# Scan gates in float32, the mixing stage's GpSimd products on VectorE, and the output turned to token rows by TensorE

## The chip, the cores and the metric

One core of one Trainium2 chip runs the kernel in one launch. The metric is the device time of that core in microseconds (us). A core has TensorE (PE in the profile, with its weight loads as PEld), VectorE (DVE), ScalarE (ACT), GpSimd (POOL) and SyncE (SP), each with an instruction queue that it works off in order; here SP issues nearly all transfers. The engines meet at semaphores.

## The reference

One layer of a bidirectional encoder: 256 tokens, 2048 features, all in float32. `rms` is an RMS norm with a gain.

```python
x = x + 0.5 * swiglu(rms(x), w1_ffn1, w3_ffn1, w2_ffn1)      # hidden width 5632
proj = rms(x) @ w_in                                         # 2048 -> 3584
q, k, v, u, y = ...                                          # 8 / 2 / 2 heads of 128; u and y 1024 wide
q, k = rope(rms(q)), rope(rms(k));  A = attention(q, k, v)   # no mask
uc = centred_conv4(u)
for each direction:                                          # forward and backward
    r = sigmoid(blockdiag(uc, w_a) + b_a)                    # 8 blocks of 128 x 128
    i = sigmoid(blockdiag(uc, w_i) + b_i)
    log_a = -8 * softplus(-lambda) * r;  a = exp(log_a)
    h[t] = a[t] * h[t-1] + sqrt(1 - a[t]**2) * i[t] * uc[t]  # scan over the tokens
x = x + concat([A, (h_fwd + h_bwd) * gelu(y)]) @ w_out
x = x + 0.5 * swiglu(rms(x), w1_ffn2, w3_ffn2, w2_ffn2)
x = x + sigmoid(rms(x) @ w_gate) * (p @ w_ple)
return rms(x)
```

The output has one row of 2048 features for each token.

## The kernel before

All 256 tokens stay in SBUF as `xs`, with the features along the partitions (16 tiles of 128 features x 256 tokens). The weights are read once from HBM, 1 MB at a time, into `raw`, of which there are three (SP issues the loads, L103). Every weight product is made in pieces of reduced float32 (fp32r): `split` (L82) cuts a half of a weight tile, 128x1024, into a high part `whi` (a cast on ACT, L83) and a low part `wlo` (a subtraction on DVE, L84); TensorE multiplies whi by the high and low part of the activations (L115, 512 columns) and wlo by the high part (L117, 256 columns). There is a ring of four pairs of whi and wlo (`SPL`), so ACT and DVE can be at most some three halves ahead of TensorE. In `proj` (L152), which makes q, k and v, the activations stand still and the weights move: three matmuls of 512 columns (L91 to L93, `mm3`) for each of eight products with a half.

The stages are the first FFN (0 to about 755 us), the mixing stage (to 965), the output projection of the mixing with `wout` (to 1051), the second FFN (to 1782), the gate with the per-layer input (to 1878) and the tail. In the mixing stage the order is: four units of u and the conv for scan group 0, four for group 1, then k and v, then two projections of q, then eight units of y. Between them run jobs, which are Python generators: `tick` (L97) takes one step of each, once after a unit and once after a quarter of a projection. The jobs are: `scan_job` (from L375) for the gates, the scans (L424, along the tokens, 128x256 each, 16 in all) and their sum `hsum`; `k_job` and `q_job` for the transposes, scores, softmax and values of the attention; `y_job` for gelu, the product with hsum and the split into `mixT`, which is the input of wout.

In the scan job the gates use mm3 too: ACT and GpSimd split the conv's output `uc` and the gate weights, and TensorE makes three fp32r matmuls of 256 columns for each of 32 products. GpSimd further makes these elementwise products of the mixing stage: us times the norm (L437), the gate times the decay constant (L407), the input gate times uc (L413), their product with the square root (L421), the sum of the directions (L427), the cosine part of the rotation (L461), and y times the norm (L574). In the whole kernel it also has the power -0.5 of the norms (L210), some products of the FFN (L304, L246) and of the gate stage.

The code gives the order in which instructions are made; a scheduler of the tile framework, which simulates the engines, then sets the order in each engine's queue. A queue is then fixed, so an instruction that waits holds all behind it.

In the tail, features 14 and 15 of the gate are done in two halves of the tokens (L651). For each half the sums of squares go through TensorE (L219), the power on GpSimd, a diagonal (L231) and a matmul (L232) that lays the norms along the free axis; DVE and GpSimd multiply xs by them (L639) and SP writes ten transfers (L641) in pieces of 512 bytes. The host puts the output into token order.

## Time and profile before

| | |
|---|---|
| runs | 1907.08, 1907.63, 1908.33 us; median 1907.63 |
| profiled execution | 1907.39 us; its span is 1905.6 us |
| PE busy | 1872.7 us, 98% of the span |
| DVE busy | 1203.6 us, 63% |
| ACT busy | 965.2 us, 51% |
| POOL busy | 292.6 us, 15% |
| mean granted clock of TensorE | 0.993 |

The profile is of one execution, and 1.8 us lie outside its span. "Busy" is the time in which an instruction runs; TensorE is pipelined, and the record of a matmul runs on for some 0.2 us after the next one has begun, so the distance between starts is the price of a matmul in a row of them. "PEclk" is the clock that TensorE was granted: 1.00 is 2.4 GHz, 0.50 is 1.2 GHz.

### The profile page before, as it was taken

The numbers are of one execution on the slowest core, as the hardware profiler recorded it, in microseconds if no ns is written. First come the engines' busy times: TensorE is split into PE (matmuls) and PEld (weight loads), VectorE is DVE, ScalarE is ACT, GpSimd is POOL, SyncE is SP. The second block draws the span as 40 slices with busy tenths as digits, with TensorE's granted clock in tenths as the row PEclk, the third lists the DMA queues.
The fourth block names the chain that finished last, engine by engine and source line by source line (L and its number), as shares of the span: only waits on it lengthen the run. The fifth ranks groups of instructions, "written<-read, shape, count | busy, mean of one in ns | idle before, by whom it ended". The sixth has DMA issues, their size and how long they took to land.

```text
span 1905.6 us, 27228 instructions
## 1 busy us (share of the span) xinstructions
PE 1872.7 (98%) x10632; PEld 1640.3 (86%) x10632; DVE 1203.6 (63%) x1723; ACT 965.2 (51%) x1494; POOL 292.6 (15%) x225
## 2 busy tenths in 40 slices
PE   9999999999999999988999999999999999999997
PEld 7888888888888888867878888888888888888886
DVE  6766655556566556888767666655555666655686
ACT  6544444444444445677654544444444444555553
POOL 0111100011111001564211111110001111101143
PEclk9999999999999999999999999999999999999998
DMA  8555545655555556544345555555565555555552
GB/s 316 205 189 187 192 160 190 210 199 179 197 180 176 182 184 213 175 152 155 133 152 181 191 185 194 182 186 167 194 208 196 181 195 184 202 197 195 201 177 67
DMA packets 61552, 352.85 MB, mean 185 GB/s; under 512 B 6512, under 2 KB 12144, under 8 KB 31088
## 3 DMA queue, kind: packets, MB, share of 16 engines
q1 hardware_dynamic: 60848, 350.51, 54.0%
q8 instruction: 83, 1.36, 0.3%
q10 hardware_dynamic: 576, 0.61, 0.1%
q14 instruction: 45, 0.37, 0.1%
HBM read 349.00 MB, written 2.10 MB: 184 GB/s over the span
## 4 chain that ended last, share of the span: by engine, by line
PE 92%; DVE 3%; ACT 3%; issue 1%; POOL 1%; DMA 0%; SPq 0%; POOLq 0%; DVEq 0%; ACTq 0%
PE acc L115 59%; PE acc L117 30%; DVE wlo L84 1%; DVE gate L424 1%; DVE uc L370 0%; ACT whi L83 0%; PE po L522 0%; PE acc L656 0%; PE pe L115 0%; POOL us L437 0%; DMA xs<-in_xT 0%; PE tr L495 0%; ACT gate L403 0%; ACT a L410 0%; ACT L416 0%
## 5 line engine op out<-in xcount | busy, mean ns | idle before, releaser
L84 DVE TENSOR_TENSOR wlo<-raw,whi 128x1024 fp32r<-128x1024 f32 x722 | 806.5, 1126 | 594.7 <-ACT whi L83 577.5
L83 ACT CAST whi<-raw 128x1024 fp32r<-128x1024 f32 x722 | 687.0, 952 | 814.5 <-PE acc L115 553.9
L115 PE MATMUL acc<-aT,whi 128*128 128x512 f32 x3296 | 832.0, 393 | 1.2 <-DVE aT L88 1.2
L115 PEld LDWEIGHTS acc<-aT,whi 128*128 128x128 f32 x3296 | 593.1, 189 | 107.8 <-DVE aT L88 2.7
L117 PEld LDWEIGHTS acc<-aT,wlo 128*128 128x128 f32 x3296 | 451.4, 191 | 32.7
L117 PE MATMUL acc<-aT,wlo 128*128 128x256 f32 x3296 | 463.0, 283 | 0.0
L115 PE MATMUL acc<-hT,whi 128*128 128x512 f32 x1408 | 364.8, 392 | 0.0
L304 POOL TENSOR_TENSOR s<-s,rB 128x256 f32<-128x256 f32 x88 | 123.8, 1407 | 1067.7 <-ACT s L301 1061.9
L115 PEld LDWEIGHTS acc<-hT,whi 128*128 128x128 f32 x1408 | 247.6, 189 | 37.2
L117 PEld LDWEIGHTS acc<-hT,wlo 128*128 128x128 f32 x1408 | 202.7, 190 | 21.3
L117 PE MATMUL acc<-hT,wlo 128*128 128x256 f32 x1408 | 209.0, 282 | 0.0
L246 POOL TENSOR_TENSOR ssq<-ssq,sqr 128x256 f32<-128x256 f32 x58 | 54.4, 939 | 339.6 <-ACT sqr L245 339.6
L115 PE MATMUL acc<-mixT,whi 128*128 128x512 f32 x256 | 64.6, 393 | 1.4 <-DVE mixT L84 1.4
L115 PEld LDWEIGHTS acc<-mixT,whi 128*128 128x128 f32 x256 | 45.9, 189 | 10.2 <-DVE mixT L84 2.1
L315 DVE SCALAR_TENSOR_TENSOR xs<-acc,xs 128x256 f32<-128x256 f32 x128 | 53.3, 417 | 0.0
L87 ACT ACTIVATE aT<-xs,par_sb 128x256 fp32r<-128x256 f32 x64 | 31.5, 506 | 41.9 <-DVE xs L315 39.3
L92 PE MATMUL acc<-wlo,aT 128*128 128x512 f32 x96 | 40.4, 421 | 11.3 <-DVE wlo L84 11.3
L88 DVE SCALAR_TENSOR_TENSOR aT<-xs,par_sb,aT 128x256 fp32r<-128x256 f32 x64 | 38.2, 610 | 19.4 <-ACT aT L87 19.1
L306 DVE TENSOR_TENSOR u<-u,s 128x256 f32<-128x256 f32 x88 | 37.4, 426 | 9.1 <-DVE u L149 0.5
L93 PE MATMUL acc<-whi,aT 128*128 128x512 f32 x96 | 39.8, 415 | 0.0
L84 DVE TENSOR_TENSOR hT<-u,hT 128x256 fp32r<-128x256 f32 x88 | 38.0, 431 | 1.9 <-ACT hT L83 1.9
L300 DVE TENSOR_TENSOR z<-z,rB 128x256 f32<-128x256 f32 x88 | 37.4, 425 | 2.7
(168 smaller groups left out, 1001.5 us busy)
## 6 DMA issues: line engine op xcount, KB each, us to landing
raw<-in_w2a SPq DMA_DIRECT2D x64, 704.0 KB, 4.0
raw<-in_w1b SPq DMA_DIRECT2D x44, 1024.0 KB, 4.8
raw<-in_w3b SPq DMA_DIRECT2D x44, 1024.0 KB, 4.9
raw<-in_w2b SPq DMA_DIRECT2D x64, 704.0 KB, 4.0
raw<-in_w3a SPq DMA_DIRECT2D x43, 1024.0 KB, 4.8
raw<-in_w1a SPq DMA_DIRECT2D x42, 1024.0 KB, 4.8
raw<-in_win SPq DMA_DIRECT2D x16, 1024.0 KB, 4.9
raw<-in_wout SPq DMA_DIRECT2D x16, 1024.0 KB, 4.8
```

Source lines behind the costliest of these rows:

```text
L83: nc.scalar.copy(hi, src)
L84: (eng or nc.vector).tensor_tensor(lo, src, f32(hi), op=ALU.subtract)
L88: nc.vector.scalar_tensor_tensor(lo, src, gain, f32(hi), op0=ALU.mult, op1=ALU.subtract)
L92: nc.tensor.matmul(ps, lhsT=ah, rhs=wl, start=False, stop=False)
L93: nc.tensor.matmul(ps, lhsT=al, rhs=wh, start=False, stop=last)
L115: nc.tensor.matmul(ps, lhsT=ws[i][0], rhs=acts[i], start=first and i == 0, stop=False)
L117: nc.tensor.matmul(ps[:, 1, :], lhsT=ws[i][1], rhs=acts[i][:, 0, :], start=False, stop=last and i == n - 1)
L246: (eng or nc.gpsimd).tensor_tensor(ssq[:, cols], ssq[:, cols], t, op=ALU.add)
L300: nc.vector.tensor_tensor(z, z, rB, op=ALU.mult)
L304: nc.gpsimd.tensor_tensor(s, s, rB, op=ALU.mult)
L306: nc.vector.tensor_tensor(u, u, s, op=ALU.mult)
L315: nc.vector.scalar_tensor_tensor(xs[:, n, :], ps[:, j, :], 0.5, xs[:, n, :], op0=ALU.mult, op1=ALU.add)
```

## The change

Four things change.

The gates of the scans (L398 now) are one plain float32 matmul for each of the 32 products, straight from `uc` and the weights as loaded; the splits of uc and of the gate weights are gone. The gate weights come by two loads of 512 KB for each group into tiles of the pool `mid`, in place of one into `raw`.

All products that GpSimd made in the mixing stage are issued to DVE. GpSimd keeps the power of the norms there.

Jobs take smaller steps and more of them: `unit` ticks after each half of the weights, `proj` after every second product of a quarter, the scan job yields in more places, and y's job is cut in two. `finish` runs the jobs to their end at two places: until hsum of a group exists before that group's y units, and all jobs before the second half of the first wout unit. The rows of wout are stored in another order (MIX_ORDER: heads 0 to 3, scan group 0, heads 4 to 7, scan group 1), and mixT is read in that order.

In the tail both halves of the tokens are finished first. Then TensorE transposes xs (32 transposes, L685), ACT and DVE scale the PSUM tiles by the token's norm, which is now a scalar for each partition (L693, L691), and SP writes eight transfers of 256 KB in rows of 2 KB (L694). The output leaves in token order.

```diff
+MIX_ORDER = [*range(4), *range(8, 12), *range(4, 8), *range(12, 16)]
...
+    def finish(done=lambda: not jobs):
+        while not done():
+            tick()
...
     def unit(aT, srcs, nk, other=None, drain=None):
...
+                if at == drain:
+                    finish()
                 unit_mms(ps, part, aT[at:at + len(part)], at == 0, at + len(part) == n)
                 at += len(part)
-        tick()
+                tick()
...
     def proj(aT, srcs):
...
-            tick()
+                if k % 2:
+                    tick()
...
     def scan_job(g, u):
-        hi = mid.tile([P, 4, S], F32R, tag="mid", name="uc_hi")
-        lo = mid.tile([P, 4, S], F32R, tag="mid", name="uc_lo")
-        split(u, hi, lo, nc.gpsimd)
-        raw = wraw.tile([P, 4, C], F32, tag="raw", name="raw")
-        in_order(nc.sync.dma_start(flat(raw), lruw[g]), loads[-1])
-        yield
         gw = []
         for d in range(2):
-            wh = mid.tile([P, 2, C], F32R, tag="mid", name="gw_hi")
-            wl = mid.tile([P, 2, C], F32R, tag="mid", name="gw_lo")
-            split(raw[:, 2 * d:2 * d + 2, :], wh, wl, nc.gpsimd)
-            gw.append((wh, wl))
+            w = mid.tile([P, 2, C], F32, tag="mid", name="gw")
+            load(flat(w), lruw[g, :, 2 * C * d:2 * C * (d + 1)])
+            gw.append(w)
         yield
...
-                        mm3(ps[:, j, :], wh[:, m, wc], wl[:, m, wc], hi[:, k, :], lo[:, k, :],
-                            True, True)
+                        nc.tensor.matmul(ps[:, j, :], lhsT=gw[d][:, m, k * P:(k + 1) * P], rhs=u[:, k, :],
+                                         start=True, stop=True)
...
-            nc.gpsimd.tensor_tensor(r[d], r[d], cb, op=ALU.mult)
+            nc.vector.tensor_tensor(r[d], r[d], cb, op=ALU.mult)
+            yield
...
-            nc.gpsimd.tensor_tensor(flat(i[d]), flat(i[d]), flat(u), op=ALU.mult)
+            nc.vector.tensor_tensor(flat(i[d]), flat(i[d]), flat(u), op=ALU.mult)
...
-            nc.gpsimd.tensor_tensor(flat(r[d]), flat(r[d]), flat(i[d]), op=ALU.mult)
+            yield
+            nc.vector.tensor_tensor(flat(r[d]), flat(r[d]), flat(i[d]), op=ALU.mult)
+            yield
             for k in range(4):
...
+                if k % 2:
+                    yield
-        nc.gpsimd.tensor_tensor(flat(i[0]), flat(i[0]), flat(i[1]), op=ALU.add)
+        nc.vector.tensor_tensor(flat(i[0]), flat(i[0]), flat(i[1]), op=ALU.add)
...
-            nc.gpsimd.tensor_tensor(t, t, rmB, op=ALU.mult)
+            nc.vector.tensor_tensor(t, t, rmB, op=ALU.mult)
...
-        nc.gpsimd.tensor_tensor(sv, sv, cb, op=ALU.mult)
+        nc.vector.tensor_tensor(sv, sv, cb, op=ALU.mult)
...
     for g in range(2):
+        finish(lambda: hsum[g] is not None)
...
-            nc.gpsimd.tensor_tensor(y[:, k, :], t, rmB, op=ALU.mult)
-        jobs.append(y_job(g, y))
-
-    tick()
+            nc.vector.tensor_tensor(y[:, k, :], t, rmB, op=ALU.mult)
+            if k % 2:
+                jobs.append(y_job(g, k // 2, y[:, k - 1:k + 1, :]))
+
+    order = [mixT[k] for k in MIX_ORDER]
...
-        ps = unit(mixT, [wout[n, 0]], NKD)
+        ps = unit(order, [wout[n, 0]], NKD, drain=8 if n == 0 else None)
...
+    def in_rows(h, b):
...
+        for k in range(4):
+            nc.tensor.transpose(ps[:, k * P:(k + 1) * P], xs[:, 4 * b + k, h * P:(h + 1) * P], ident)
+        return ps
+
+    def put(h, b, ps, r):
+        o = tok.tile([P, C], F32, tag="att", name="out", bufs=ATT)
+        if b % 2:
+            nc.vector.tensor_scalar(o, ps, r, None, op0=ALU.mult)
+        else:
+            nc.scalar.activation(o, ps, AF.Copy, scale=r)
+        nc.sync.dma_start(out[h * P:(h + 1) * P, b * C:(b + 1) * C], o)
+
+    last_features(0)
+    last_features(1)
+    r0 = norms(0)
+    for b in range(4):
+        put(0, b, in_rows(0, b), r0)
+    ahead = [in_rows(1, b) for b in range(3)]
+    r1 = norms(1)
+    for b in range(3):
+        put(1, b, ahead[b], r1)
+    put(1, 3, in_rows(1, 3), r1)
```

The queues outside the mixing stage and the tail keep their order on every engine. In the queues below a number behind a name tells one buffer from another, and a name's last `<-` has what is read.

On DVE, before, at the projections of k, v and q: the gates of scan group 0 (`a` is the decay, `gate` the gates and, later, the scan's results) come in four rows of scans among the subtractions for the weights.

```order
L419 SCALAR_TENSOR_TENSOR gate_7240<-a_7496,gate_7240 128x1024
L419 SCALAR_TENSOR_TENSOR gate_7375<-a_7500,gate_7375 128x1024
L84 TENSOR_TENSOR wlo_7694<-raw_7691,whi_7693 128x1024
L424 SCALAR_TENSOR_TENSOR gate_7310<-a_7496,gate_7240 128x256 x4
L84 TENSOR_TENSOR wlo_7698<-raw_7691,whi_7697 128x1024
L424 SCALAR_TENSOR_TENSOR gate_7434<-a_7500,gate_7375 128x256 x4
L84 TENSOR_TENSOR wlo_7753<-raw_7750,whi_7752 128x1024
L209 TENSOR_SCALAR rs_v_7586<-qss_7581 128x2
L84 TENSOR_TENSOR wlo_7757<-raw_7750,whi_7756 128x1024
```

On DVE, after, at the same place; the products that GpSimd made stand among them (L414 and L407 of group 1, L423 of group 0).

```order
L88 TENSOR_TENSOR wlo_7574<-raw_7571,whi_7573 128x1024
L420 SCALAR_TENSOR_TENSOR gate_7128<-a_7421,gate_7128 128x1024
L414 TENSOR_TENSOR gate_7425<-gate_7425,uc_7080 128x1024
L423 TENSOR_TENSOR gate_7128<-gate_7128,gate_7190 128x1024
L420 SCALAR_TENSOR_TENSOR gate_7288<-a_7453,gate_7288 128x1024
L88 TENSOR_TENSOR wlo_7578<-raw_7571,whi_7577 128x1024
L427 SCALAR_TENSOR_TENSOR gate_7190<-a_7421,gate_7128 128x256 x4
L88 TENSOR_TENSOR wlo_7629<-raw_7626,whi_7628 128x1024
L423 TENSOR_TENSOR gate_7288<-gate_7288,gate_7348 128x1024
L88 TENSOR_TENSOR wlo_7633<-raw_7626,whi_7632 128x1024
L407 TENSOR_TENSOR gate_7500<-gate_7500,cneg_6844 128x1024
L427 SCALAR_TENSOR_TENSOR gate_7348<-a_7453,gate_7288 128x256 x2
```

Four scans still stand between two subtractions, and three more products of 128x1024 stand among six subtractions.

On PE, before, where wout begins (two units run side by side, acc_8662 and acc_8710): the transposes of the last softmax (`pt`, L513) and the values (`po`, L522) stand after the third of the eight pairs of input tiles of mixT. mixT_7618, which L115 reads in the last row, has heads 6 and 7, the outcome of po_8544.

```order
L115 MATMUL acc_8710<-mixT_7617,whi_8713 128x512 x2
L513 MATMUL tr_8475<-ident_102,pt_8409 128x128
L513 MATMUL tr_8482<-ident_102,pt_8409 128x128
L513 MATMUL tr_8475<-ident_102,pt_8421 128x128
L513 MATMUL tr_8475<-ident_102,pt_8409 128x128
L513 MATMUL tr_8475<-ident_102,pt_8421 128x128
L513 MATMUL tr_8482<-ident_102,pt_8421 128x128
L513 MATMUL tr_8482<-ident_102,pt_8409 128x128
L513 MATMUL tr_8482<-ident_102,pt_8421 128x128
L522 MATMUL po_8544<-pT_sb_8480,v_sb_7337 128x256 x2
L522 MATMUL po_8544<-pT_sb_8487,v_sb_7337 128x256 x2
L115 MATMUL acc_8662<-mixT_7618,whi_8665 128x512 x2
```

On PE, after, at the same place, with the values of heads 4 and 5 (po_8218) and the scores (L499) and transposes (L517) of heads 6 and 7; mixT_7561, 7562 and 7565 hold heads 0 to 3 and the first pair of scan group 0.

```order
L526 MATMUL po_8218<-pT_sb_8193,v_sb_7323 128x256 x2
L499 MATMUL tr_8225<-kT_7560,qT_8104 128x256 x2
L499 MATMUL tr_8237<-kT_7560,qT_8104 128x256 x2
L526 MATMUL po_8218<-pT_sb_8200,v_sb_7323 128x256 x2
L517 MATMUL tr_8280<-ident_102,pt_8231 128x128
L517 MATMUL tr_8287<-ident_102,pt_8231 128x128
L123 MATMUL acc_8574<-mixT_7565,whi_8577 128x512 x2
L123 MATMUL acc_8626<-mixT_7565,whi_8629 128x512 x2
L517 MATMUL tr_8280<-ident_102,pt_8243 128x128
L517 MATMUL tr_8280<-ident_102,pt_8231 128x128
L517 MATMUL tr_8280<-ident_102,pt_8243 128x128
L517 MATMUL tr_8287<-ident_102,pt_8243 128x128
```

Behind these rows stand two more transposes, four matmuls of the values of heads 6 and 7 (po_8314), and only then the unit goes on, with mixT_7566 (the second pair of scan group 0). What the first half of wout reads is no longer made by the last values, but the last values still stand ahead of it in PE's queue.

On DVE, before, at the very end: the norm of the first half (rs_v, dg), the last features, three products for the output, then the second half's norm and five more products.

```order
L231 TENSOR_SCALAR dg_17157<-ident_102,inv_17153 128x128
L615 TENSOR_TENSOR small_17097<-small_17097,pe_17036 128x128
L616 TENSOR_TENSOR xs_83<-xs_83,small_17097 128x128
L620 TENSOR_TENSOR last_17060<-xs_83 128x128
L639 TENSOR_TENSOR xs_83<-xs_83,rows_17161 128x4x128 x3
L621 TENSOR_SCALAR xs_83<-xs_83,par_sb_82 128x128
L209 TENSOR_SCALAR rs_v_17222<-sums_17217 128x1
L231 TENSOR_SCALAR dg_17225<-ident_102,inv_17221 128x128
L639 TENSOR_TENSOR xs_83<-xs_83,rows_17226 128x2x128 x2
L639 TENSOR_TENSOR xs_83<-xs_83,rows_17226 128x4x128 x3
```

On DVE, after, at the very end: four scalings of transposed tiles (`out`), of 128 tokens by 512 features each, wait for the norms and the transposes alone; ACT has the other four.

```order
L221 TENSOR_SCALAR rs_v_17122<-sums_17118 128x1
L662 TENSOR_TENSOR sqr_17113<-xs_83 128x128
L664 TENSOR_TENSOR last_16975<-last_16975,sqr_17113 128x128
L667 TENSOR_SCALAR xs_83<-xs_83,par_sb_82 128x128
L691 TENSOR_SCALAR out_17138<-out_17133,inv_17121 128x512
L691 TENSOR_SCALAR out_17154<-out_17149,inv_17121 128x512
L221 TENSOR_SCALAR rs_v_17176<-sums_17172 128x1
L691 TENSOR_SCALAR out_17182<-out_17162,inv_17175 128x512
L691 TENSOR_SCALAR out_17193<-out_17188,inv_17175 128x512
```

The diagonal and its matmul are gone, and no product waits for a GpSimd product.

## Rows read from the trace of the kernel before

**Rows 1.** Windows: busy us (and instructions) of each engine, clock, DMA share, GB/s.
```profile
core 0: us, PE busy (x) PEld busy (x) DVE busy (x) ACT busy (x) POOL busy (x), PEclk, DMA share, GB/s
830.00:893.00 63.00, 49.97 (x200) 38.99 (x201) 54.13 (x56) 40.56 (x77) 34.46 (x17) 0.89 0.34 117
951.00:965.00 14.00, 9.40 (x40) 6.75 (x40) 8.12 (x19) 10.33 (x20) 0.72 (x1) 0.88 0.22 75
965.00:1051.00 86.00, 86.00 (x498) 75.82 (x497) 60.88 (x77) 44.01 (x62) 13.96 (x14) 1.00 0.54 183
```

**Rows 2.** Waits of PE from 755 to 1051: total us, times, longest.
```profile
PE acc L92 <- DVE wlo L84: 11.3, 5, 4.7
PE tr L513 <- DVE pt L506: 2.3, 2, 1.8
```

**Rows 3.** Timeline, 829 to 846: start, us, engine, operation, idle before it.
```profile
831.01 1.21 DVE L84 TENSOR_TENSOR wlo<-raw,whi 128x1024 fp32r<-128x1024 f32 x1
831.23 3.23 POOL L421 TENSOR_TENSOR gate<-gate 128x1024 f32<-128x1024 f32 x1 [1.23 <-DVE gate L419]
832.14 6.74 DVE L424 TENSOR_TENSOR_SCAN gate<-a,gate 128x256 f32<-128x256 f32 x4
834.21 0.63 PE L92 MATMUL acc<-wlo,aT 128*128 128x512 f32 x1
834.64 0.63 PE L93 MATMUL acc<-whi,aT 128*128 128x512 f32 x1
...
839.92 2.42 DVE L424 TENSOR_TENSOR_SCAN gate<-a,gate 128x256 f32<-128x256 f32 x4
...
840.06 0.80 PE L92 MATMUL acc<-wlo,aT 128*128 128x512 f32 x1 [3.17 <-DVE wlo L84]
```

**Rows 4.** Timeline, 874 to 894: the scans of group 1.
```profile
875.27 6.69 DVE L424 TENSOR_TENSOR_SCAN gate<-a,gate 128x256 f32<-128x256 f32 x4
...
883.13 0.80 PE L92 MATMUL acc<-wlo,aT 128*128 128x512 f32 x1 [4.72 <-DVE wlo L84]
```

**Rows 5.** DVE's groups, 755 to 965: busy us, mean ns, idle before.
```profile
L84 DVE TENSOR_TENSOR wlo<-raw,whi 128x1024 fp32r<-128x1024 f32 x55 | 80.9, 1485 | 20.5 <-ACT whi L83 16.6 <-ACT pT_sb L515 2.0 <-ACT rB L236 1.5
L424 DVE TENSOR_TENSOR_SCAN gate<-a,gate 128x256 f32<-128x256 f32 x16 | 18.3, 1199 | 0.0
...
L419 DVE SCALAR_TENSOR_TENSOR gate<-a,gate 128x1024 f32<-128x1024 f32 x4 | 7.3, 1818 | 5.9 <-ACT gate L416 5.9
...
L149 DVE TENSOR_TENSOR ys<-acc,ys 128x256 f32<-128x256 f32 x8 | 3.4, 419 | 0.2
```

**Rows 6.** GpSimd's group L421 of the same stretch.
```profile
L421 POOL TENSOR_TENSOR gate<-gate 128x1024 f32<-128x1024 f32 x4 | 12.2, 3062 | 15.1 <-DVE gate L419 12.0 <-PE acc L93 3.1
```

**Rows 7.** ACT's groups of the same stretch.
```profile
L403 ACT ACTIVATE gate<-tr,par_sb 128x256 f32<-128x256 f32 x32 | 12.6, 477 | 0.0
...
L410 ACT ACTIVATE a<-gate 128x1024 f32<-128x1024 f32 x4 | 4.0, 1052 | 0.0
L403 ACT ACT_TABLE_LOAD x3 | 3.8, 1283 | 0.1
```

**Rows 8.** PE's timeline, 799.5 to 801.5: gate matmuls.
```profile
800.61 0.28 PE L91 MATMUL tr<-uc_hi,gw_hi 128*128 128x256 f32 x1
800.72 0.28 PE L92 MATMUL tr<-uc_lo,gw_hi 128*128 128x256 f32 x1
```

**Rows 9.** PE's timeline, 905 to 925: four float32 matmuls of the values, four of scores.
```profile
911.62 1.89 PE L522 MATMUL po<-pT_sb,v_sb 128*128 128x256 f32 x8
913.35 1.89 PE L495 MATMUL tr<-kT,qT 128*128 128x256 f32 x8
```

**Rows 10.** Timeline of the tail, 1882 to the end.
```profile
1889.99 0.84 PE L656 MATMUL acc<-aT,whi 128*128 128x256 f32 x5
...
1893.47 2.36 POOL L639 TENSOR_TENSOR xs<-xs,rows 128x256 f32<-128x256 f32 x2 [1.41 <-ACT rows L666]
...
1898.56 2.54 DVE L639 TENSOR_TENSOR xs<-xs,rows 128x256 f32<-128x256 f32 x5 [0.95 <-PE rows L232]
```

**Rows 11.** A window of the tail (columns as in rows 1).
```profile
1902.00:1904.00 2.00, 0.00 (x0) 0.00 (x0) 0.00 (x0) 0.00 (x0) 0.00 (x0) 0.50 0.90 282
```

More of the change, by code (lines that the diff above doesn't have):

```diff
@@ L129, in weights, with unit @@
         return got
-    def unit(aT, srcs, nk, other=None):
+    def unit(aT, srcs, nk, other=None, drain=None):
         if other is not None:
@@ L210, in rsqrt, with inv_rms, spread @@
         nc.gpsimd.tensor_tensor(dst, v, mhalf[:, :width], op=ALU.pow)
-    def inv_rms(*ssq, halves=range(NH), keep=True):
+    def inv_rms(*ssq):
         ps = trp.tile([P, 2, S], F32, tag="tr", name="sums")
-        n = len(halves)
-        for i, h in enumerate(halves):
+        for h in range(NH):
             for j, s in enumerate(ssq):
-                nc.tensor.matmul(ps[:, 0, i:i + 1], lhsT=s[:, h * P:(h + 1) * P], rhs=ones[:, 0:1],
+                nc.tensor.matmul(ps[:, 0, h:h + 1], lhsT=s[:, h * P:(h + 1) * P], rhs=ones[:, 0:1],
                                  start=j == 0, stop=j == len(ssq) - 1)
-        return spread(ps[:, 0, :n], n, keep)
-    def spread(sums, n=NH, keep=True):
-        r = sml.tile([P, NH], F32, tag="inv", name="inv", bufs=2)[:, :n]
-        rsqrt(r, sums, D, n)
+        return spread(ps[:, 0, :NH])
+    def spread(sums):
+        r = sml.tile([P, NH], F32, tag="inv", name="inv", bufs=2)
+        rsqrt(r, sums, D, NH)
         dg = tmp("dg")
         pb = trp.tile([P, 2, S], F32, tag="tr", name="rows")
-        for i in range(n):
-            cols = slice(i * P, (i + 1) * P)
-            nc.vector.tensor_scalar(dg[:, cols], ident, r[:, i:i + 1], None, op0=ALU.mult)
+        for h in range(NH):
+            cols = slice(h * P, (h + 1) * P)
+            nc.vector.tensor_scalar(dg[:, cols], ident, r[:, h:h + 1], None, op0=ALU.mult)
             nc.tensor.matmul(pb[:, 0, cols], lhsT=ones, rhs=dg[:, cols], start=True, stop=True)
-        if not keep:
-            return r, pb[:, 0, :n * P]
         rB = sml.tile([P, S], F32, tag="rB", name="rB", bufs=2)
@@ L556, in hymba_layer, with y_job @@
         jobs.append(q_job(qc, qro, qsc))
[L559 to L565 removed]
+    def y_job(g, b, part):
+        nc.scalar.activation(part, part, AF.Gelu_apprx_tanh)
+        nc.vector.tensor_tensor(part, part, hsum[g][:, 2 * b:2 * b + 2, :], op=ALU.mult)
+        dst = mix2[4 + 2 * g + b]
+        split(part, dst[:, :, 0, :], dst[:, :, 1, :])
         yield
     for g in range(2):
+        finish(lambda: hsum[g] is not None)
         y = mtile("y")
@@ L650, in hymba_layer, with last_features @@
         small.append(t)
-    for h in range(NH):
+    def last_features(h):
         cols = slice(h * P, (h + 1) * P)
+        pss = []
         for i in range(2):
@@ L661, in hymba_layer @@
             nc.vector.tensor_tensor(g, g, rpB[:, cols], op=ALU.mult)
-            gated(n, g, pe[i], cols, nc.vector, last[i])
-        _, rf = inv_rms(ssq3, *last, halves=[h], keep=False)
-        if h == 0:
-            rows = tmp("rows")[:, :P]
-            nc.scalar.copy(rows, rf)
-            scale_out(0, rows, 0, nc.gpsimd)
-        else:
-            scale_out(0, rows, 1, nc.vector)
-            scale_out(1, rf, 0, nc.vector)
-            scale_out(1, rf, 1, nc.vector)
+            x = xs[:, n, cols]
@@ new lines, in last_features @@
+            nc.scalar.activation(g, g, AF.Sigmoid)
+            nc.vector.tensor_tensor(g, g, pe[i][:, cols], op=ALU.mult)
+            nc.vector.tensor_tensor(x, x, g, op=ALU.add)
+            t = last[:, cols] if i == 0 else tmp("sqr")[:, cols]
+            nc.vector.tensor_tensor(t, x, x, op=ALU.mult)
+            if i == 1:
+                nc.vector.tensor_tensor(last[:, cols], last[:, cols], t, op=ALU.add)
+        for i in range(2):
+            x = xs[:, NKD - 2 + i, cols]
+            nc.vector.tensor_scalar(x, x, par_at(O_GF + NKD - 2 + i), None, op0=ALU.mult)
@@ new lines, in norms @@
+    def norms(h):
+        cols = slice(h * P, (h + 1) * P)
+        ps = trp.tile([P, 2, S], F32, tag="tr", name="sums")
+        for j, q in enumerate((ssq3, last)):
+            nc.tensor.matmul(ps[:, 0, 0:1], lhsT=q[:, cols], rhs=ones[:, 0:1], start=j == 0, stop=j == 1)
+        r = sml.tile([P, NH], F32, tag="inv", name="inv", bufs=2)[:, :1]
+        rsqrt(r, ps[:, 0, :1], D, 1)
+        return r
+    def in_rows(h, b):
+        if b % 2:
+            ps = trp.tile([P, C], F32, tag="tr", name="out")
+        else:
+            ps = acc.tile([P, C], F32, tag="acc", name="out")
+        for k in range(4):
+            nc.tensor.transpose(ps[:, k * P:(k + 1) * P], xs[:, 4 * b + k, h * P:(h + 1) * P], ident)
+        return ps
@@ L759 @@
     r = run_bass_kernel_spmd(nc, [sent], core_ids=[0])
[L760 to L761 removed]
+    return r.results[0]["out_0"].reshape(1, S, D)
```

59 lines of the change are left out of this document (19 added, 40 removed).

## The prediction

> **What bounds the kernel now.** I read the windows first, then TensorE's waits, then the timeline at each wait, then the groups of the engines that are waited for.
>
> Over long stretches TensorE never stops: from 965 to 1051 it is busy for all 86.00 us, at full clock [rows 1]. The change touches nothing there, and the queues outside the mixing stage and the tail keep their order, so I look for the gain only where TensorE stands still. In the mixing stage that is in two places: 830 to 893, where it is idle for 63.00 - 49.97 = 13.0 us, and 951 to 965, with 14.00 - 9.40 = 4.6 us. In both the clock is below full (0.89 and 0.88) [rows 1].
>
> The waits say for what: 11.3 us in five waits of L92 for a subtraction wlo on DVE [rows 2], all of them in the first place. The timeline says why the subtraction is late. At 832.14 four scans take 6.74 us, while four others of the same size at 839.92 take 2.42; GpSimd's product L421 runs for 3.23 us from 831.23, beside the slow ones. The next subtraction stands behind the scans, and TensorE waits 3.17 us for it, until 840.06 [rows 3]. The same at 875.27 (6.69 us for four scans) and 883.13 (idle 4.72 us) [rows 4]. Before and after these stops the matmuls start 0.43 us apart (834.21 and 834.64 [rows 3]), which is the lower clock of 1.2 GHz; at 2.4 GHz it is half of that. I count 26 such matmuls, 0.2 us too much each: 5 us. A stop also costs 0.2 to 0.3 us more than its idle time, since the record of the last matmul runs on: about ten stops, 2.5 us. So the first place loses 13.0 + 5 + 2.5 = about 20 us, and the second, reckoned alike (4.6 idle, 1.7 by the clock, the rest restarts), about 8.
>
> In the second place TensorE waits for the last softmax (L506) [rows 2] and what follows it, a chain through four engines.
>
> **The change part by part.** The profiled execution took 1907.4 us, of which 1905.6 are the span; the median is 0.2 above it. All terms are set against 1907.4.
>
> *The products that leave GpSimd.* They go to DVE: 14 of 128x1024 (four each of L407, L413, L421, two of L427), 16 of 128x256 (us and y), four of 128x512 and two of 128x256 in the rotation. A subtraction of 128x1024 that nothing disturbs takes 1.21 us [rows 3] and an addition of 128x256 0.42 [rows 5]; for 128x512 I take 0.7, between them. So 14 x 1.2 + 16 x 0.42 + 4 x 0.7 + 2 x 0.42 = 27 us more for DVE. What it gets back: the subtractions took 1.485 us in the mean, 55 x (1.485 - 1.21) = 15 us; the scans 1.199 instead of 2.42 / 4 = 0.605, 16 x 0.59 = 9.5 us; L419 1.82 instead of some 1.2, 2.5 us [rows 3, 5]. That is 27 us too. DVE's load stays about equal, but nothing then holds an instruction for 6.7 us, and GpSimd's 3.06 us for L421 [rows 6] become 1.2 in the chain that leads to the scans.
>
> The rows show that DVE is slow where GpSimd works; they don't show whether all of the stretch is GpSimd's doing. The Trainium skill (SBUF — State Buffer, Who interferes with whom) says that a VectorE instruction with two SBUF inputs and a GpSimd instruction that reads SBUF lock each other out for the whole instruction; scans that take 6.74 instead of 2.42 us beside a GpSimd product agree. By that rule all 27 us come back, by a mere sharing of one path perhaps half.
>
> *Is DVE then in time?* In the order of DVE after, the four subtractions from wlo_7574 to wlo_7633 have between and behind them six operations of 128x1024 (L420, L414, L423, L407) and six scans: after the first, 3 x 1.2 + 6 x 1.2 + 6 x 0.6 = 14.4 us. A half of the weights lasts TensorE 2.7 us (16 matmuls in a half of a unit at 86.00 / 498 = 0.173 us [rows 1]; a projection's half has as many columns). Three halves and the gate matmuls between them are about 11.5 us. DVE falls 3 us behind there and some 5.5 us over six halves; the ring of four lets it be three halves ahead, 8 us. DVE alone should stop nothing.
>
> *ACT.* In the same stretch its new order has seven table loads of 1.28 us, six passes over 128x1024 and five casts of the same size at 1.05, ten sigmoids at 0.48 [rows 7] and four smaller copies of about 0.47: 9 + 11.6 + 4.8 + 1.9 = 27 us, against five halves and the gates on TensorE, 13.5 + 10 x 0.43 = 18. ACT falls 9 us behind, a little more than the ring covers. Two cast tiles late are 2 to 4 us of stop, and a stop brings the lower clock for a while, 1 to 2 us. Bounds for what is left at this place: 0 (the ring full when it begins) and 20 (as now). I take 5: **-15 us**.
>
> *Gates in float32.* Out go 96 fp32r matmuls that start 0.11 to 0.12 us apart [rows 8], 11.5 us; in come 32 of float32, of the shape of the values and scores, which show as two records each, 0.216 us apart ((913.35 - 911.62) / 8 [rows 9]): 64 x 0.216 = 13.8. **+2.3 us**, all on TensorE. Twelve ACT passes for the high parts go as well (six of 128x1024), and GpSimd's low parts. The Trainium skill (FP8 and Floating Point Precision, TensorE Precision Notes) counts four passes for true float32; with each pass as long as an fp32r matmul here the sum would be 128 x 0.12 = 15.4, that is +3.9; the records say two slower passes, and I go by them. The loads of the gate weights are the same bytes in two transfers for one; SP's queue has few, and the DMA engines are busy for 0.34 of their time there [rows 1]. I cost that at nothing.
>
> *The start of wout.* The chain behind the last scores is the same: maximum, four exponentials, scaling, transposes, a copy of PSUM, values, the split. What changes is that the four matmuls of po_8218 and wout's pair mixT_7565 stand in it to be done meanwhile, about 8 x 0.216 + 4 x 0.23 = 2.6 us, and that y's split no longer comes last. Against it: finish() puts all jobs ahead of the second half, and the last values still stand before mixT_7566 in PE's queue. 8 becomes 5.5: **-2.5 us**; bounds -5 (the whole idle time) and +2 (two chains in a row).
>
> *The tail.* Before, TensorE's last big matmul ends at 1890.83, the last product at 1901.10, the span at 1905.6 [rows 10]; GpSimd's product of 2.36 us at 1893.47 [rows 10] holds the second norm. After, 32 transposes run in some 3.5 us beside the last norms; the first scaling can be done some 3.6 us after the last matmul, the last one 6.3 after it. So the transfers decide: 2.1 MB at 282 GB/s, the rate in the last window [rows 11], are 7.4 us; at 183 / 0.54 = 339 GB/s, what the weights' rate makes at a full share [rows 1], 6.2. With 1 us until the first bytes and 1.9 us behind the last (both as now), the end comes 12.7 to 13.9 us after the last matmul, against 14.8. Five fewer matmuls for sums and rows between give 0.3. **-2 us**; bounds -4 and +0.5.
>
> Sum: -15 + 2.3 - 2.5 - 2 = -17.2, and 1907.4 - 17.2 = 1890.2: 1890 us.
>
> **The rivals.** (a) *The stretch is not GpSimd's, or DVE's new work takes its place.* For it: DVE is busy for 54.13 of 63 us already [rows 1], and its queue is in order, so a product that waits for a sigmoid holds the subtractions behind it. Against it: 6.74 and 2.42 us for the same four scans. The stops stay at 20 us: 1907.4 + 2.3 - 2.5 - 2 = about 1905, no change that counts.
>
> (b) *Slower: waits across ACT and DVE.* L407, L414 and L420 on DVE each wait for ACT's sigmoids, exponentials or roots, and those wait in turn behind table loads and for TensorE's gates; the subtractions stand behind them in DVE's row. GpSimd took that wait on itself for L407 and L413. If such a wait lasts longer than the 8 us of the ring, it stops TensorE in each of some seven such places, for as long as the worst now (4.72 us [rows 4]): 33 us in place of 20, and 1907.4 + 13 + 2.3 - 2.5 - 2 = 1918 us. It decides from some 23 us of stops on. Against it: smaller steps of the jobs put fewer of these into a row.
>
> (c) *Nothing stops any more.* The ring is full when the scans begin, the stops of the first place vanish (-20), wout's start keeps 4 us of the 8 and the tail gains 3: 1907.4 - 20 - 4 - 3 + 2.3 = 1883 us. For it: products like L421, 3.06 us on GpSimd [rows 6], are gone from the chains that feed the scans. Against it: ACT's sum above.
>
> (d) *The tail is bound by its transfers as before*, at 282 GB/s and with no gain: the forecast at 1892.
>
> **How the numbers follow.** The forecast has 0.55, with (d) 0.10 on its upper side; (c) has 0.18, (a) 0.09, (b) 0.08. The likeliest is 1890. Its own range is 1885 to 1898 (stops of 0 to 12 us at the scans). With (c) below and half of (a) above, 8 in 10 lie from 1881 to 1903. A measurement tells about 0.2%, 3.8 us, from no change. Faster by more than that are the forecast, (c), (d) and a small part of (a): 0.86; within it is most of (a): 0.07; slower is (b): 0.07.
>
> **What would show it.** Right: the scans' group at 0.6 to 0.7 us in the mean and the 128x1024 subtractions at 1.2 over the mixing stage; TensorE's waits for wlo there under 4 us in sum; gate matmuls as 64 records some 0.216 apart; the clock at 1.00 between 800 and 950; first output transfer about 4 us after the last L649. Wrong: scans or subtractions of 2 us or more with GpSimd at rest; a wait of TensorE for wlo behind L407 or L420 of 4 us or more, or for ACT's casts behind table loads; a new idle stretch of 8 us or more at the second half of the first wout unit; tail transfers that begin early and end as late as before.

## The result and the profile after

| | before | after |
|---|---|---|
| median of the runs, us | 1907.98 (1907.08 to 1908.74, 4 runs) | 1889.72 (1889.62 to 1890.84, 4 runs) |
| profiled execution, us; span | 1907.39; 1905.6 | 1889.62; 1887.8 |
| PE, DVE, ACT, POOL busy, us | 1872.7, 1203.6, 965.2, 292.6 | 1870.6, 1185.3, 963.1, 213.2 |
| mean granted clock | 0.993 | 0.999 |

The ratio is 0.9906, with a 95% interval of 0.9889 to 0.9923: 18 us less, where 17 were forecast (1890). To see where they come from I cut both profiled executions at the starts of the same matmuls: the last of the first FFN, the last of wout, the last of the second FFN, the first of the last two features' low-part products (L647, now L638) and the last of their large ones (L656, now L649).

| us | before | after | difference |
|---|---|---|---|
| up to the end of the first FFN | 746.60 | 747.29 | +0.7 |
| mixing stage and wout | 304.11 | 289.06 | -15.05 |
| second FFN, gate | 737.84, 90.15 | 737.84, 90.15 | 0 |
| last features | 11.84 | 11.40 | -0.44 |
| from the start of the last large matmul to the end | 15.05 | 12.10 | -2.95 |

The first row is no effect of the change: that stretch is the same code and took 746.6 to 748.7 us in all the kernels below.

First the windows of the kernel after, with the columns of [rows 1]. wout begins at 935 now, so the second row is the place that answers to 951 to 965.

```profile
830.00:893.00 63.00, 60.35 (x280) 48.45 (x279) 55.50 (x86) 49.32 (x99) 11.94 (x6) 1.00 0.52 184
...
930.00:951.00 21.00, 16.57 (x89) 13.48 (x88) 13.04 (x30) 13.95 (x32) 0.00 (x0) 1.00 0.28 101
...
965.00:1051.00 86.00, 86.00 (x498) 75.83 (x497) 59.43 (x76) 42.72 (x60) 14.84 (x15) 1.00 0.54 185
```

At the scans TensorE is idle for 2.65 us instead of 13.0, and the clock does not fall. At wout's start it is idle for 4.43 us, about what it was (4.6), but at full clock. TensorE's waits in the same stretch, which answer to [rows 2]:

```profile
PE acc L123 <- DVE mixT L88: 2.8, 2, 2.0
PE acc L96 <- DVE wlo L88: 2.6, 4, 1.3
PE tr L517 <- DVE pt L510: 1.2, 1, 1.2
```

The 11.3 us for wlo have become 2.6, the longest 1.3. DVE's timeline there, for [rows 3]:

```profile
830.50 1.22 DVE L88 TENSOR_TENSOR wlo<-raw,whi 128x1024 fp32r<-128x1024 f32 x1
831.63 2.43 DVE L427 TENSOR_TENSOR_SCAN gate<-a,gate 128x256 f32<-128x256 f32 x4
833.98 1.20 DVE L88 TENSOR_TENSOR wlo<-raw,whi 128x1024 fp32r<-128x1024 f32 x1
835.10 1.21 DVE L423 TENSOR_TENSOR gate<-gate 128x1024 f32<-128x1024 f32 x1
836.23 1.21 DVE L88 TENSOR_TENSOR wlo<-raw,whi 128x1024 fp32r<-128x1024 f32 x1
```

DVE has no gap here: it works without a break, but each instruction takes what it takes alone, the scans 2.43 us for four where they took 6.74.

Not every scan was slow before. Here are all 16 before, and then after (ns: least, median, most):

```profile
L424 DVE TENSOR_TENSOR_SCAN gate<-a,gate x16: 657/659/2881, 832.1 to 886.0; 128x256 f32<-128x256 f32 x16
```

```profile
L427 DVE TENSOR_TENSOR_SCAN gate<-a,gate x16: 658/667/686, 831.6 to 874.6; 128x256 f32<-128x256 f32 x16
```

Before, two of the first four scans were long, and [rows 3] leaves out a second product of GpSimd beside them:

```profile
832.14 2.87 DVE L424 TENSOR_TENSOR_SCAN gate<-a,gate 128x256 f32<-128x256 f32 x1
...
836.10 2.79 DVE L424 TENSOR_TENSOR_SCAN gate<-a,gate 128x256 f32<-128x256 f32 x1
```

```profile
835.89 2.44 POOL L413 TENSOR_TENSOR gate<-gate,uc 128x1024 f32<-128x1024 f32 x1 [1.43 <-ACT gate L403]
```

L421 ends at 834.46 and the first scan 0.55 us later; L413 ends at 838.33 and the other long scan 0.56 later. The two scans between them take 0.66 us each. So a scan was not slowed down: it stood until the product was over and then took about its own time. Five of the 16 were held so, for 1.0 to 2.2 us each. The groups from 755 to 965, beside [rows 5]:

```profile
L88 DVE TENSOR_TENSOR wlo<-raw,whi 128x1024 fp32r<-128x1024 f32 x61 | 74.0, 1220 | 22.7 <-ACT whi L87 19.6 <-ACT rB L245 1.5 <-PE acc L125 1.0
L427 DVE TENSOR_TENSOR_SCAN gate<-a,gate 128x256 f32<-128x256 f32 x16 | 9.8, 669 | 0.0
...
L423 DVE TENSOR_TENSOR gate<-gate 128x1024 f32<-128x1024 f32 x4 | 4.9, 1217 | 0.0
L420 DVE SCALAR_TENSOR_TENSOR gate<-a,gate 128x1024 f32<-128x1024 f32 x4 | 4.8, 1224 | 3.3 <-ACT gate L417 3.3
```

Subtractions 1485 to 1220 ns, scans 1199 to 669, L419 (now L420) 1818 to 1224. L423, 3062 ns on GpSimd [rows 6], takes DVE 1217.

The gates on PE, in four products at a time, have the two records each and the 0.216 us of [rows 9]:

```profile
809.11 1.89 PE L398 MATMUL tr<-uc,gw 128*128 128x256 f32 x8
```

The tail's timeline, for [rows 10]:

```profile
1868.19 7.84 PE L649 MATMUL acc<-aT,whi 128*128 128x256 f32 x64
1876.01 1.83 PE L685 MATMUL out<-ident,xs 128*128 128x128 f32 x15
1878.93 1.41 DVE L691 TENSOR_SCALAR out<-out,inv 128x512 f32<-128x512 f32 x2
1879.64 5.49 SPq L694 DMA_DIRECT2D out<-out  x8
1884.02 0.75 DVE L691 TENSOR_SCALAR out<-out,inv 128x512 f32<-128x512 f32 x1 [0.67 <-DMA out<-out]
```

And a window of it, for [rows 11]:

```profile
1880.50:1882.00 1.50, 0.00 (x0) 0.00 (x0) 0.00 (x0) 0.18 (x1) 0.54 (x1) 1.00 1.01 376
```

The first scaling comes 2.9 us after the last large matmul, the first transfer 3.6 us. The transfers then run at 376 GB/s in this window, and at 358 and 335 in the two behind it, not at the 282 of [rows 11].

### The profile page after: what moved, and what is told of

The parts are those of the page before. It is cut to its first block, busy times and chain, and to the rows that moved or that the text cites. A ratio compares the mean times of both kernels' runs of the same rounds, so it can differ in the third digit from the quotient of the medians.

```text
span 1887.8 us, 27190 instructions
## 1 busy us (share of the span) xinstructions
PE 1870.6 (99%) x10624; PEld 1638.2 (87%) x10624; DVE 1185.3 (63%) x1755; ACT 963.1 (51%) x1491; POOL 213.2 (11%) x181
## 4 chain that ended last, share of the span: by engine, by line
PE 96%; ACT 2%; DVE 1%; DMA 1%; issue 0%; SPq 0%; POOL 0%; ACTq 0%; DVEq 0%
PE acc L123 60%; PE acc L125 31%; PE acc L96 0%; PE tr L398 0%; DMA xs<-in_xT 0%; PE acc L97 0%; PE acc L649 0%; PE pe L123 0%; PE acc L95 0%; PE po L526 0%; PE tr L499 0%; DVE wlo L88 0%; DVE gate L427 0%; ACT a L411 0%; ACT L411 0%
## 5 line engine op out<-in xcount | busy, mean ns | idle before, releaser
L88 DVE TENSOR_TENSOR wlo<-raw,whi 128x1024 fp32r<-128x1024 f32 x722 | 792.4, 1105 | 594.7 <-ACT whi L87 577.4
L310 ACT ACTIVATE s<-z 128x256 f32<-128x256 f32 x88 | 36.4, 413 | 4.3 <-DVE z L309 4.3
```

The source lines that it names most:

```text
L88: (eng or nc.vector).tensor_tensor(lo, src, f32(hi), op=ALU.subtract)
L310: silu = nc.scalar.activation(s, z, AF.Silu)
```

## The experiments

All twelve kernels are set against the kernel before on their own chip; the lengths of a stage come from the profiled executions, cut as above. Where a kernel is "the changed kernel with", it is to be read against 1889.72 us, 289.1 us for the mixing stage with wout, and 12.10 us for the tail.

| run | median, us | ratio to before, 95% interval | mixing and wout | tail |
|---|---|---|---|---|
| e1 products back on GpSimd | 1907.05 | 0.9995 (0.9986 to 1.0005) | 306.0 | 12.1 |
| e2 before, products moved only | 1892.12 | 0.9916 (0.9902 to 0.9931) | 289.7 | 14.8 |
| e3 extra GpSimd reading | 1907.08 | 0.9996 (0.9985 to 1.0006) | 305.7 | 12.1 |
| e4 extra GpSimd writing | 1893.01 | 0.9922 (0.9902 to 0.9941) | 292.0 | 12.15 |
| e5 gates in three, GpSimd | 1890.85 | 0.9915 (0.9902 to 0.9929) | 290.7 | 12.3 |
| e6 wout's start as before | 1889.57 | 0.9905 (0.9890 to 0.9920) | 288.2 | 12.1 |
| e7 before, new tail only | 1905.73 | 0.9987 (0.9978 to 0.9996) | 303.6 | 12.3 |
| e8 tail in 512 bytes | 1892.36 | 0.9921 (0.9909 to 0.9933) | 291.9 | 13.5 |
| e9 gates in three, DVE | 1890.74 | 0.9914 (0.9899 to 0.9928) | 288.9 | 12.2 |
| e10 more buffers in the tail | 1889.88 | 0.9913 (0.9896 to 0.9930) | 289.1 | 11.8 |
| e11 three units ahead | 1891.61 | 0.9920 (0.9905 to 0.9935) | 290.5 | 12.1 |
| e12 e6, e9 and e10 together | 1889.92 | 0.9907 (0.9890 to 0.9923) | 288.4 | 12.0 |

**e1: the products back.**

```diff
-            nc.vector.tensor_tensor(flat(r[d]), flat(r[d]), flat(i[d]), op=ALU.mult)
+            nc.gpsimd.tensor_tensor(flat(r[d]), flat(r[d]), flat(i[d]), op=ALU.mult)
...
```

and so for L407, L414, L431, L441, L465 and L577.

> The changed kernel with its seven kinds of elementwise products of the mixing stage back on GpSimd; float32 gates, smaller job steps, wout's order and the new tail stay. Theory (GpSimd's products hold DVE's instructions): the scans' mean goes from 0.67 us back to 1.0 or more, TensorE's stops between 826 and 893 us from 3.8 us to 10 to 16, time 1896 to 1904 us. Rival (the smaller steps and the float32 gates, which take 24 us of splitting from GpSimd, did it): stops stay under 6 us, time under 1892 us.

The whole gain is gone, more than I expected: 1907.05 us, although float32 gates, small steps and the new tail all stay. The rival falls. Its mechanism is the one forecast, but not the form: the scans were hardly stretched (0.73 us in the mean), the operations beside them were. Timeline of e1 where TensorE waits longest:

```profile
866.67 3.32 POOL L423 TENSOR_TENSOR gate<-gate 128x1024 f32<-128x1024 f32 x1 [7.72 <-DVE gate L420]
...
867.64 3.43 DVE L420 SCALAR_TENSOR_TENSOR gate<-a,gate 128x1024 f32<-128x1024 f32 x1
...
871.00 4.67 DVE L464 TENSOR_TENSOR sq<-qs,tabs 128x256 f32<-128x256 f32 x4
...
875.59 3.44 DVE L427 TENSOR_TENSOR_SCAN gate<-a,gate 128x256 f32<-128x256 f32 x4
...
878.96 2.33 DVE L88 TENSOR_TENSOR wlo<-raw,whi 128x1024 fp32r<-128x1024 f32 x2
...
880.20 0.80 PE L96 MATMUL acc<-wlo,aT 128*128 128x512 f32 x1 [8.15 <-DVE wlo L88]
```

L420, L464 and the scans, 5.1 us in the changed kernel (1.22, 1.43 and 2.43), take 11.4 us from 867.64 on, and the subtraction is last in the row. Which of DVE's instructions is held depends on what stands beside a GpSimd product; that one is held does not.

**e2: the move alone.** The same seven edits the other way, in the kernel before.

> The kernel before with only the seven kinds of products moved to DVE; gates in three fp32r matmuls with GpSimd's splits, the old job steps, wout's order and tail stay. Theory: the scans are at 0.6 to 0.7 us and most of the 20 us lost between 826 and 893 go, 10 to 16 us of them: 1892 to 1898 us. Rival (the move alone is not enough, the steps are needed, since four scans and two products of 128x1024 then stand between subtractions): 1900 us or more.

1892.12 us: 15.6 of the 18 us come from the move of the products by itself. The rival falls; with the old steps TensorE is idle only 63.00 - 59.89 = 3.1 us from 830 to 893. DVE's groups in e2:

```profile
L84 DVE TENSOR_TENSOR wlo<-raw,whi 128x1024 fp32r<-128x1024 f32 x61 | 75.9, 1258 | 18.4 <-ACT whi L83 16.7 <-ACT rB L236 1.5
L424 DVE TENSOR_TENSOR_SCAN gate<-a,gate 128x256 f32<-128x256 f32 x16 | 9.8, 675 | 0.0
```

**e3 and e4: company that reads, and company that writes.**

```diff
             nc.vector.tensor_tensor(flat(r[d]), flat(r[d]), flat(i[d]), op=ALU.mult)
+            nc.vector.tensor_copy(u[:, 0, 0:1], r[d][:, 0, 0:1])
+            for _ in range(2):                                      # e4: range(4)
+                nc.gpsimd.tensor_tensor(flat(u), flat(u), flat(u), op=ALU.subtract)   # e4: nc.gpsimd.memset(flat(u), 0.0)
```

> The changed kernel with eight extra GpSimd subtractions of 128x1024 (uc minus itself, when uc is no longer needed; nothing waits for their outcome), two behind each product L423, so that they run beside the scans; a DVE copy of 128x1 starts them. They read SBUF. Theory (the lock): the scans and subtractions beside them take 2 to 3 times as long, TensorE's stops grow by 4 to 12 us, time 1894 to 1902 us. Rival (what cost before was the way of the data through GpSimd, not the company): scans stay at 0.67 us, time within 2 us of 1889.7.

> As the run with extra GpSimd subtractions, but sixteen GpSimd memsets of 128x1024 in their place, four behind each product: about as much GpSimd time, written and not read. If reading SBUF is what collides with DVE's second input, the scans stay at 0.67 us and the time at 1889 to 1892 us; if any GpSimd work beside DVE stretches it, the time is that of the run with subtractions. Both runs put the same delay on the small powers that queue behind on GpSimd.

The two tell most of all. e3, whose extra GpSimd work nobody waits for, loses the gain again, 17.4 us, more than the theory gave. First e3, then e4, at the first scans:

```profile
831.72 5.73 DVE L430 TENSOR_TENSOR_SCAN gate<-a,gate 128x256 f32<-128x256 f32 x4
...
831.98 4.35 POOL L426 TENSOR_TENSOR uc<-uc 128x1024 f32<-128x1024 f32 x2 [74.89 <-DVE uc L424]
...
838.63 0.50 PE L96 MATMUL acc<-wlo,aT 128*128 128x512 f32 x1 [3.83 <-DVE wlo L88]
```

```profile
832.79 2.43 DVE L430 TENSOR_TENSOR_SCAN gate<-a,gate 128x256 f32<-128x256 f32 x4
...
833.02 4.00 POOL L426 MEMSET uc<- 128x1024 f32 x4 [74.88 <-DVE uc L424]
...
836.39 0.50 PE L96 MATMUL acc<-wlo,aT 128*128 128x512 f32 x1 [0.54 <-DVE wlo L88]
```

GpSimd is busy for about as long beside the same four scans. Reading SBUF, it makes 5.73 us of them; writing alone, it leaves them at 2.43. So what holds the scans is neither GpSimd's slowness in the chain of data nor its being busy; it is that it reads. The Trainium skill (SBUF — State Buffer, Who interferes with whom) says just this: a VectorE instruction with two SBUF inputs contends with a GpSimd instruction that reads SBUF, not with one that only writes it. The runs agree with it for the scans and subtractions. Beside e4's memsets three other instructions were held, for 1.7 us in all: small ones (tensor_scalar), one of L481 and two of L560. L560 in the changed kernel (there L557), then in e4:

```profile
L557 DVE TENSOR_SCALAR qsc<-qrs 128x4 f32<-128x4 f32 x4 | 0.7, 168 | 1.8 <-POOL qrs L222 1.8
```

```profile
L560 DVE TENSOR_SCALAR qsc<-qrs 128x4 f32<-128x4 f32 x4 | 1.6, 400 | 1.5 <-POOL qrs L222 1.5
```

So work on GpSimd that only writes is not free beside every instruction of DVE. e4 is 3 us slower than the changed kernel, a little outside the range I gave, but not here: between 826 and 893 its stops sum to 4.0 us against 3.8. Its profile has the lower clock at wout's start instead (see the last section).

**e5 and e9: the gates in three fp32r matmuls.** In the changed kernel, with the splits' low parts on GpSimd (e5) or on DVE (e9).

```diff
-                        nc.tensor.matmul(ps[:, j, :], lhsT=gw[d][:, m, k * P:(k + 1) * P], rhs=u[:, k, :],
-                                         start=True, stop=True)
+                        mm3(ps[:, j, :], gw[d][0][:, m, wc], gw[d][1][:, m, wc], hi[:, k, :], lo[:, k, :],
+                            True, True)
...
+        split(u, hi, lo, nc.gpsimd)                                  # e9: nc.vector
...
+            split(raw[:, 2 * d:2 * d + 2, :], wh, wl, nc.gpsimd)     # e9: nc.vector
```

> The changed kernel with the scans' gates as before: three fp32r matmuls, high parts on ACT, low parts on GpSimd (six subtractions, 17 us), weights through one load into raw. All else as changed. Theory (the float32 gates only cost TensorE time: 64 records of 0.216 against 96 of 0.12): 2.3 to 2.5 us less, 1887.0 to 1887.6 us, since GpSimd's splits fall mostly into the units of u, where DVE has room. Rival (GpSimd's splits hold DVE's instructions, so the float32 gates pay for themselves): 1889.5 us or more.

> The changed kernel with the scans' gates in three fp32r matmuls, as in the run before it of that kind, but the six low parts subtracted on DVE instead of GpSimd. It parts the two causes there. If GpSimd's splits holding DVE ate the 2.4 us that TensorE saves, they come out now: the stops between 826 and 893 stay under 4.5 us with the clock loss under 0.7, mixing stage and wout 286.5 to 287.5 us, time 1887 to 1888. If the splitting itself (ACT's and DVE's work, 13 us) is what costs: 289 us or more, time 1889.5 or more.

My theory for e5 fell: no 2.4 us came out. In e9, which takes GpSimd's splits out of the company, they did not come out either (288.9 us against 289.1), so the splits on GpSimd are not what ate them. Nor did either of e9's two outcomes come whole: its stops at the scans (4.1 us, clock loss 0.4) are those of the first, its time those of the second. In both runs TensorE waits 2.5 us at once for wlo, where the changed kernel's longest such wait is 1.3 (e9):

```profile
PE acc L96 <- DVE wlo L88: 3.4, 2, 2.5
```

and in both profiles the clock at wout's start is 0.93 over 928 to 953, where the changed kernel's is 1.00. Against 2.4 us fewer of matmuls stand 1.4 (e9) and 1.6 us (e5) more of stops over the whole stage. The lower clock costs each another 1.5 at wout's start, and e5 another 1.0 between 830 and 893, where it falls to 0.97. The clock at wout's start can differ from one execution to the next (last section); whether it does so here by chance is not shown, since all eight executions of e5 and e9 have a mean clock of 0.995 to 0.998, and three of the changed kernel's four have 0.999. Without it the gates in three matmuls would be worth 1 us at most, too little for these medians to tell: the float32 gates neither cost nor save time that can be seen.

**e6: wout's start as before.** No finish(), no MIX_ORDER; the smaller steps stay.

```diff
-        finish(lambda: hsum[g] is not None)
...
-        ps = unit(order, [wout[n, 0]], NKD, drain=8 if n == 0 else None)
+        ps = unit(mixT, [wout[n, 0]], NKD)
```

> The changed kernel without finish() at its two places and with wout's rows and mixT in the old order; job steps, float32 gates, products and tail stay. Theory (the new start of wout saves about 3 us, as the run with the products alone moved, which lost 9 us there, against 5.6, suggests): 1891.5 to 1894 us. Rival (the smaller steps alone give it): within 1 us of 1889.7.

I expected 3 us from the order and the draining; there are none. The stage is 0.85 us shorter without them, and the medians are the same. The rival stands: what is gained at wout's start does not come from these two edits.

**e7: the new tail in the kernel before.** Lines L610 to L671 replaced by those of the changed kernel, and the output's layout with them.

> The kernel before with the new tail alone. Theory: the tail's share of the gain, 3.4 us (0.4 before the last large matmul, 3.0 behind it), stands by itself: 1904.0 to 1904.6 us. Rival (part of it came from elsewhere): 1906 us or more.

Ratio 0.9987 (0.9978 to 0.9996): 2.5 us less by the medians, 3.2 by the profile (last features and tail 26.89 to 23.65 us). The tail's gain stands by itself. The median is 1.1 us above the range I gave, which the interval still reaches. Some 0.6 us of that lies outside the spans: by the medians of the spans, 1906.3 and 1903.2 us, the gain is 3.1.

**e8 and e10: the size of the pieces, and the buffers.**

```diff
-        nc.sync.dma_start(out[h * P:(h + 1) * P, b * C:(b + 1) * C], o)
+        nc.sync.dma_start(out[h, b].rearrange("e p f -> p e f"), o.rearrange("p (e f) -> p e f", f=P))   # e8
...
-        o = tok.tile([P, C], F32, tag="att", name="out", bufs=ATT)
+        o = mid.tile([P, 2, C], F32, tag="mid", name="out")[:, 0, :]                                     # e10
```

> The changed kernel with its eight output transfers written in pieces of 512 bytes, as before, in place of rows of 2 KB. If the rows of 2 KB are what lifts the rate in the tail from some 285 to 380 GB/s, the end comes 1.2 to 1.8 us later: 1891 to 1891.6 us. Rival (512 bytes already run at line rate and the earlier supply of data is what helped): within 0.4 us of 1889.7, and 370 GB/s or more in the tail's windows.

> The changed kernel with the tail's eight scaled tiles in the 17 buffers of another pool instead of four, so that no scaling waits for a transfer (four of eight did, 0.7 to 2.2 us each). Theory (the transfers' rate, some 380 GB/s, sets the end and the waits are behind it): the tail goes from 12.05 to 11.5 to 11.8 us. Rival (the waits hold the last transfer): 11.2 us or less.

In windows of the tail, e8 first and then e10 (columns as in [rows 1]):

```profile
1885.00:1887.00 2.00, 0.00 (x0) 0.00 (x0) 0.34 (x1) 0.69 (x1) 0.00 (x0) 1.00 1.02 286
```

```profile
1881.00:1885.00 4.00, 0.00 (x0) 0.00 (x0) 1.41 (x2) 1.27 (x2) 0.16 (x1) 0.84 1.03 380
```

The DMA engines have no free time in either (1.02 and 1.03), but 512-byte pieces make 286 GB/s of it and 2 KB rows 380. e8's tail is 13.54 us, 1.44 more, inside what the theory gave; its median is 2.6 us more, above the range. Its profiled execution took 5.1 us more, of which 2.9 lie in the mixing stage and wout, by the clock (last section), and 0.8 in the first FFN. The pieces are those of before: the traces count 4224 packets in e8's tail, 4256 before and 1152 after. More buffers take away every wait for a transfer and 0.3 us: the rate sets the end. The Trainium skill (DMA: Bandwidth & Descriptors, Specifications) has 512 bytes as the smallest transfer at line rate; here it was not, and the measurement decides.

**e11: more ready work at wout's start.** The first halves of three units stand ahead of finish(), four input tiles at a time.

```diff
+    for n in range(3):
...
+        half(raw, ps, 0)
+        tick()
+    finish()
+    for n, (raw, ps) in enumerate(begun_units):
+        half(raw, ps, 8)
+        mixed(n, ps)
```

> The changed kernel with the first halves of three wout units instead of one ahead of finish(), each made four input tiles at a time, so that some 20 more matmuls that wait for none of the last values stand in the row beside the last softmax. Theory (TensorE stops there for want of ready work): the 5.7 us lost at wout's start fall to 2.5 to 4, time 1886.5 to 1888.5. Rival (the chain over ACT gets longer by the casts of the further weights, so that the end of the last values moves): no less than 5 us lost, time within 1 us of 1889.7.

No gain, though not for the rival's reason. The last scores on PE, in the changed kernel and then in e11:

```profile
938.13 1.89 PE L499 MATMUL tr<-kT,qT 128*128 128x256 f32 x8
```

```profile
939.66 1.89 PE L526 MATMUL po<-pT_sb,v_sb 128*128 128x256 f32 x8
941.39 1.89 PE L499 MATMUL tr<-kT,qT 128*128 128x256 f32 x8
```

The scheduler put most of the extra matmuls ahead of the scores in PE's queue; only some ten matmuls of wout stand behind them. The chain that follows began 3.3 us later, and the stops are 5.3 us, where the changed kernel has 5.1. So what more ready work behind the scores would be worth is not shown.

**e12: three edits together.**

> The changed kernel with three of the edits tried: gates in three fp32r matmuls with all splits off GpSimd, neither finish() nor the new order of wout, and the tail's tiles in more buffers. Sum of what the single runs' profiles showed against the changed kernel: -2.4 us of matmuls and about +1.2 of stops for the gates, -0.9 at wout, -0.2 in the tail: 1887.0 to 1888.0 us if they add up. Rival (the jobs' schedule shifts with every edit and the stops with it): 1889 us or more.

The rival: 1889.92 us, no better than the changed kernel. No version that I ran beats it by more than the noise (e6's median is 0.15 us lower).

## Why the prediction was right

The mechanism was right, and the time (1890 forecast, 1889.7 measured) is the sum of terms that each came out within 1.5 us. That the sum is so close is luck in part: the scans and the tail gave 2.4 us more than forecast, the gates and wout's start 1.1 less, and the first FFN, which the change doesn't touch, took 0.7 longer. The losses are read as in the prediction: the stops with their restarts, and the matmuls at the lower clock.

- *Scans, -15 us.* Lost between 826 and 893: 14.7 us of stops, 5.1 by the clock and 0.6 besides before, 20.4 in all; after, 3.8 and 0.6: -16. The prediction set the slow scans beside L421 alone; L413 held the second of them. Each hold lasts until the product ends, as by the rule of the whole instruction that the prediction went by, and not by a mere sharing. That GpSimd's reading holds DVE is shown by e3 against e4, that the move does it by e1 and e2.
- *DVE's load stays equal.* Mis-sized, though it did no harm. DVE's busy time fell by 18.3 us with 27 more to do: with 2.7 us less in the tail, some 42 us of holding went, not 27. I had counted three groups; others were held as well, the conv's L370 (now L379) from 617 to 480 ns and short ones, L553 (now L557) from 716 to 168 ns, L474 (now L478) from 811 to 280.
- *ACT falls 9 us behind.* The stop that I took from it (2 to 4 us) is what is left, by size, but it comes another way. No wait for ACT's casts is among TensorE's there, all four are for wlo on DVE, and "DVE alone should stop nothing" failed. DVE in the changed kernel, with ACT's cast for the last row, which ends 2.1 us before that subtraction begins:

```profile
826.97 1.23 DVE L414 TENSOR_TENSOR gate<-gate,uc 128x1024 f32<-128x1024 f32 x1 [0.93 <-ACT gate L403]
...
837.84 1.04 ACT L87 CAST whi<-raw 128x1024 fp32r<-128x1024 f32 x1
...
840.97 1.21 DVE L88 TENSOR_TENSOR wlo<-raw,whi 128x1024 fp32r<-128x1024 f32 x1
```

  From 826.97 on DVE has no gap until past 843, and three of the four stops fall into that stretch: the subtractions stand behind DVE's other work, in a row that starts late because L414 waits for a sigmoid on ACT. How much of it is ACT's share no run shows.
- *Float32 gates, +2.3 us.* Matmuls of the stage, summed by their undisturbed distances: 276.1 to 278.6 us, +2.5. Four passes of 0.12 us each would have been +3.9; the two records, 0.43 us for each matmul, gave the better price. How many passes lie in a record they don't tell.
- *wout's start, -2.5 us.* 7.2 us lost before, 5.6 after: -1.6, of which only 0.4 are stops (5.5 to 5.1). The rest is the clock, which between e8 and the changed kernel differs by more, so the size is not settled. The reason given failed: I put it on the values and the pair that stand in the chain and on y's split, which come with finish() and the order of wout. e6 has neither and loses 4.8. y's split does come last, behind the split of the values, and TensorE waits for it:

```profile
948.38 0.69 DVE L88 TENSOR_TENSOR mixT<-po,mixT 128x512 fp32r<-128x512 f32 x1 [2.72 <-ACT mixT L87]
948.99 0.68 DVE L88 TENSOR_TENSOR mixT<-y,mixT 128x512 fp32r<-128x512 f32 x1
949.72 0.73 PE L123 MATMUL acc<-mixT,whi 128*128 128x512 f32 x2 [2.00 <-DVE mixT L88]
```

  In e6, whose unit goes on with the heads, TensorE's waits for mixT are 1.6 us instead of 2.8. What remains for the gain are the smaller steps and y's job in pairs, which no run had alone.
- *Tail, -2 us.* Mis-sized: -3.4. The step that failed is the rate, for which I took 282 to 339 GB/s; it was 335 to 376, and e8 shows that the size of the pieces is the reason. The other steps held: first scaling done some 3.6 us after the last large matmul, as forecast, and the sums between worth 0.44 (0.3). The last scaling was done after 8.7 us, not 6.3, as four of the eight wait for a buffer; e10 shows that this costs 0.3 us.

Rival (a) falls by e2 and e3, (b) by the waits (the longest for wlo is 1.3 us, where it needed some 4.7), (d) by the tail's rate. Of (c) one of three parts came true: the tail.
